# The b21 product of two column pairs, split once more by Strassen's scheme

## The chip, the cores and the metric

The kernel runs on one core of a Trainium2 chip. Its time is the device time of that core in microseconds (us). Three runs of the kernel before took 1364.69 to 1365.26 us, median 1365.02 us.

## What is computed

One layer of a decoder trunk on a sequence of 1024 rows and 1024 features. The input is normalized and modulated (`h`), and one large projection gives all branches; everything is float32.

```python
h = rms_norm(x, norm_w) * (1 + scale) + shift
proj = h @ w_in            # (1024 x 1024) @ (1024 x 11296)
gm_u, gm_v, gm_z, ssm_z, xbc, dt_raw, g_a, g_b = split(proj)
y_a = spatial_gating(gelu(gm_u), gelu(gm_v), ...) * silu(gm_z)
xbc = silu(causal_depthwise_conv(xbc, conv_w, conv_b))
y_b = rms_norm((ssd_scan(...) + xs * d_skip) * silu(ssm_z))
merged = sigmoid(g_a) * (y_a @ w_proj_a) + sigmoid(g_b) * (y_b @ w_proj_b)
out = rms_norm(x + gate * (merged @ w_out), final_norm_w)
```

The change concerns `h @ w_in` alone, and of it the columns other than gm_v, dt_raw and the first two blocks of g_a.

## The kernel before

**Column pairs.** The columns of `w_in` are taken in blocks of 128, two blocks (c1, c2) at a time: 39 pairs. A pair is a matrix product with 2 x 2 blocks: the 1024 contracted rows are halved, the 1024 sequence positions are halved, and the two column blocks are the other side. `pair` (from L590) takes it by seven products in place of eight, with sums of blocks on both sides. The sums of the sequence side (b11, t1, t2, b22, t3, b21, t4; tiles `bop`) are the same for all pairs and stay in SBUF. The sums of the weight side are made for each pair by `pair_weights` (L554) from four loaded quarters: a11, a21, a22, a12 and s1, s2, s4 in eight "ws" buffers.

**Float32 by parts.** Every operand is split into a rounded part and the rest ("h" and "l": a copy on ACT, L571, and a subtraction on DVE, L572), and a product is h x h, h x l and l x h. So `product` (L580) issues 3 x 4 = 12 matmuls of 128 x 128 weights and 512 columns into one PSUM bank. The parts of the weights lie in two rings of eight tiles.

**Order of a pair.** p1, p5, then the p4 of the pair before, p6, p3, p2, p7. p1, p6, p7 and p4 add up in one bank (px), p5 and p3 in another (py), p2 has its own (pz) and uses a12 and b21. ACT copies or DVE adds what stands in a bank into c1 and c2, the results of both column blocks (L601, L637), and then `done1` and `done2` work on them: the convolution (`conv_done`), gates (`z_done`, `gate_done`), or for gm_z and gm_u the "uz" pairs (`zg_done`, `u_done`, L1039 to L1050). The sixteen first pairs are a convolution pair and a uz pair in turn.

**Queues.** Every matmul and every load is kept in the order of the program on its queue (`pin`): PE for matmuls, SP's queue for all loads. Stores go out on ACT's queue. The order on ACT, DVE and POOL is set by a planner with a model of costs; evacuations of PSUM are put ahead (`tc.high_priority`). Side work is hung into a count of products (`later`, `run_tasks`): the mixing weights of the gate, the loads vm (mixing input of a uz pair, `mix_load`), ag and wog (output gates), wbr (weights of the second projection).

**Room.** c1, c2, the convolution's ac, vm, ag and others share six tiles of 128 x 1024, "w4" (`wide`). PSUM in this stage has a px tag of two banks and a "bk" tag of six. After the 37 pairs of `jobs` come two more (`tail`), then the state-space part, the projections and the output. The sequence side's tiles are used again there as room for other tiles.

## Time and profile before

| what | value |
|---|---|
| median of 3 runs | 1365.02 us |
| profiled execution | 1362.27 us |
| its span, first to last instruction | 1360.4 us |
| PE busy | 1347.0 us (99%), 6907 matmuls and transposes |
| weight loads (PEld) | 1114.4 us (82%) |
| DVE busy | 1056.1 us (78%) |
| ACT busy | 800.4 us (59%) |
| POOL busy | 196.1 us (14%) |
| bytes moved by DMA | 288.64 MB, mean 212 GB/s |

PE is TensorE's matmuls, PEld its weight loads (they overlap matmuls), DVE VectorE, ACT ScalarE, POOL GpSimd, SP the queue of loads. The column pairs lie between 143 us and about 905 us of the span. Matmuls are pipelined: the record of one of 512 columns is 389 ns long, and the next one starts 227 ns after it, so the pace is read from the starts. In a row of instructions the columns are start, length, engine, line, operation, output and inputs, shapes and count; behind "[" is the idle time of the engine before it and what ended it. In a row of a group the busy time is followed by the mean length in ns.

### The profile page before, as it was taken

What the parts mean: (1) busy time and instruction counts of PE and PEld (TensorE: products, weight loads), DVE (VectorE), ACT (ScalarE), POOL (GpSimd) and SP (SyncE); (2) the same over time, 40 slices, a digit from 0 to 9 for tenths busy, and PEclk for the clock granted to TensorE, in tenths of its full rate; (3) what the DMA queues carried; (4) which work ended last, traced back from release to release, by engine and by line L of the source; (5) the groups of instructions that cost most, each with busy time, mean ns of one, the idle gap of its engine ahead of it and who ended that gap; (6) DMA issues with size and microseconds to landing.
All of it is one profiled execution on the core that took longest, in us unless ns stands there. A gap on an engine that the chain in (4) does not pass through costs nothing.

```text
span 1360.4 us, 20108 instructions
## 1 busy us (share of the span) xinstructions
PE 1347.0 (99%) x6907; PEld 1114.4 (82%) x6907; DVE 1056.1 (78%) x1731; ACT 800.4 (59%) x1446; POOL 196.1 (14%) x193
## 2 busy tenths in 40 slices
PE   8999999999999999999999999999999999999997
PEld 6688888888888888888888888888888888888886
DVE  4776786787777898688887788358888877959976
ACT  5754666666657665466576655486877834233453
POOL 1000000000000000000000000007798981000002
PEclk9999999999999999999999999999999999999999
DMA  9675444333345667777656866489889878888913
GB/s 292 177 248 142 134 124 124 117 119 122 101 132 155 193 184 231 248 216 246 202 192 193 244 204 186 154 289 318 302 297 311 306 256 291 313 261 317 381 45 124
DMA packets 249577, 288.64 MB, mean 212 GB/s; under 512 B 16860, under 2 KB 196484, under 8 KB 249476
## 3 DMA queue, kind: packets, MB, share of 16 engines
q1 hardware_dynamic: 174868, 203.80, 47.0%
q10 hardware_dynamic: 74544, 83.57, 18.0%
q8 instruction: 54, 0.88, 0.3%
q14 instruction: 47, 0.39, 0.1%
q0 software_dynamic: 64, 0.00, 0.0%
HBM read 199.82 MB, written 87.49 MB: 211 GB/s over the span
## 4 chain that ended last, share of the span: by engine, by line
PE 93%; POOL 3%; DMA 1%; issue 1%; ACT 1%; DVE 1%; SPq 0%; POOLq 0%; DVEq 0%; ACTq 0%
PE xcb L585 6%; PE xz L585 6%; PE xuz L585 6%; PE xx L585 6%; PE xg L585 6%; PE pma L82 5%; PE ox L1914 3%; PE yuz L585 3%; PE yx L585 3%; PE ycb L585 3%; PE yp L1722 3%; PE yz L585 3%; PE vx L990 3%; PE yg L585 3%; PE oy L1914 2%; PE x0p L1722 2%
## 5 line engine op out<-in xcount | busy, mean ns | idle before, releaser
L1159 POOL TENSOR_SCALAR_AFFINE_SELECT dcy<-dcy 128x1024 f32<-128x1024 f32 x32 | 35.3, 1103 | 788.7 <-ACT ea L1155 788.7
L1167 ACT ACTIVATE dcy<-dcy,nacs 128x128 f32<-128x128 f32 x256 | 78.3, 389 | 2.9 <-POOL dcy L1159 2.4
L1183 DVE TENSOR_TENSOR dcy<-dcy,pc 128x1024 f32<-128x1024 f32 x32 | 39.0, 1218 | 8.0 <-PE pc L85 5.8
L1265 POOL TENSOR_TENSOR yz<-y,sl 128x512 f32<-128x512 f32 x32 | 44.7, 1396 | 2.5
L82 PE MATMUL pma<-yh,wah 128*128 128x512 f32 x128 | 43.2, 418 | 0.0
L82 PE MATMUL pma<-yh,wal 128*128 128x512 f32 x128 | 42.6, 413 | 0.0
L82 PE MATMUL pma<-yl,wah 128*128 128x512 f32 x128 | 40.2, 395 | 0.0
L1155 ACT ACTIVATE ea<-dcy 64x512 f32<-64x512 f32 x64 | 39.8, 622 | 0.4
L1190 ACT COPY bn<-pc 128x256 f32<-128x256 f32 x32 | 11.9, 371 | 46.4 <-DVE dcy L1183 44.9
L1060 ACT ACTIVATE ac<-ac 128x1024 f32<-128x1024 f32 x32 | 33.9, 1060 | 8.1 <-DVE ac L1058 7.9
L1264 POOL TENSOR_TENSOR y<-y,ym 128x512 f32<-128x512 f32 (+1 forms) x32 | 37.4, 1170 | 1.8 <-DVE ym L1262 1.8
L1058 DVE SCALAR_TENSOR_TENSOR ac<-c2x,cwt,ac 128x1023 f32<-128x1023 f32 (+2 forms) x24 | 30.7, 1278 | 8.8 <-ACT ac L1056 8.7
L1058 DVE SCALAR_TENSOR_TENSOR ac<-c2cb,cwt,ac 128x1023 f32<-128x1023 f32 (+2 forms) x24 | 30.7, 1278 | 8.2 <-ACT ac L1056 8.0
L1929 POOL TENSOR_TENSOR r<-r,fnw 128x512 f32<-128x512 f32 x4 | 6.1, 1534 | 207.3 <-ACT junk L1927 207.3
L82 PE MATMUL yi<-dcy,xd 128*64 128x128 f32 x512 | 35.0, 279 | 0.0
L1262 DVE TENSOR_TENSOR ym<-yn,ea 128x512 f32<-128x512 f32 (+1 forms) x32 | 19.9, 621 | 18.2 <-PE yn L82 18.0
L1653 DVE SCALAR_TENSOR_TENSOR yn<-yn,par,rb 128x512 f32<-128x512 f32 x32 | 26.1, 822 | 9.1 <-DMA yn<-yb_d 9.1
L82 PE MATMUL sp<-xe,bn 128*128 128x256 f32 x112 | 32.7, 409 | 0.0
L82 PEld LDWEIGHTS yn<-sl,st 128*128 128x128 f32 x224 | 29.8, 191 | 2.8 <-POOL st L1228 0.4
L82 PEld LDWEIGHTS yi<-dcy,xd 128*64 128x64 f32 x512 | 27.3, 136 | 5.7 <-issue 3.2
L1058 DVE SCALAR_TENSOR_TENSOR ac<-c1cb,cwt,ac 128x1023 f32<-128x1023 f32 (+2 forms) x24 | 30.6, 1276 | 1.3 <-ACT ac L1056 1.3
L1022 ACT ACTIVATE vm<-vm,vr 128x128 f32<-128x128 f32 x64 | 25.5, 483 | 10.1 <-DMA vm<-v_d 9.6
(2983 smaller groups left out, 4368.4 us busy)
## 6 DMA issues: line engine op xcount, KB each, us to landing
sl<-s_d SPq DMA_DIRECT2D x32, 768.0 KB
s_d<-ac ACTq DMA_DIRECT2D x32, 512.0 KB
wb_d<-wbb ACTq DMA_DIRECT2D x32, 512.0 KB
dcy<-acs_d SPq DMA_DIRECT2D x32, 512.0 KB
av<-in_w_in_dram SPq DMA_DIRECT2D x36, 256.0 KB
aw<-in_ada_w_dram SPq DMA_DIRECT2D x16, 512.0 KB
wbr<-in_w_proj_b_dram SPq DMA_DIRECT2D x32, 256.0 KB
yb_d<-yz ACTq DMA_DIRECT2D x32, 256.0 KB
```

Of the source, the lines that this page charges most:

```text
L82: pin(PE.matmul(acc, l, r, start=first, stop=last))
L585: pin(PE.matmul(ps, lw[:, k * P : (k + 1) * P], r[k], start=first and n + k == 0, stop=n == 2 and k == 3, skip_group_check=not first))
L990: pin(PE.matmul(ps[pn][j], l[:, j * P : (j + 1) * P], r, start=nm in ("p1", "p5", "p2") and n + units[i][1] == 0, stop=n == 2 and k == 3, ...
L1058: V.scalar_tensor_tensor(ac[:, s:], cc[:, : S - s], conv_wt[:, 3 - s, i : i + 1], ac[:, s:], op0=ALU.mult, op1=ALU.add)
L1155: link("A", lambda: A.activation(ea[hh * HD : (hh + 1) * HD], dcy.rearrange("p (j e) i l -> p e j (i l)", e=2)[hh * HD : (hh + 1) * HD, hh ...
L1159: link("G", lambda: G.affine_select(out=d8, in_=d8, compare_op=ALU.is_ge, fill=-1e30, base=0, pattern=[[0, 2 * HPG], [1, P]], channel_mult ...
L1167: link("A", lambda: A.activation(dcy[:, h, i, :], dcy[:, h, i, :], AF.Exp, bias=sub[:, i, h : h + 1]))
L1183: link("V", lambda: V.tensor_tensor(d3, d3, pc[:, 0:256].unsqueeze(1).to_broadcast([P, HPG, 256]), op=ALU.mult))
L1264: link("G", lambda: G.tensor_add(y1[:, :, t0:], y1[:, :, t0:], m[:, :, t0:]))
L1265: link("G", lambda: G.tensor_mul(yz, y1, sl[:, 4:6]))
L1722: pin(PE.matmul(ps[j], a[:, v, js], r, start=first and n + k == 0, stop=n == 2 and k == KT - 1, skip_group_check=not first))
L1914: pin(PE.matmul(ps, a[:, tsl], b[:, cs], start=first and n + j == 0, stop=n == 2 and j == 3, skip_group_check=not first))
```

## The change

For 34 of the 39 pairs, from the fourth to the 37th, two pairs in a row ("a" and "b", 17 times) share their p2. The a12 of a and the a12 of b stand side by side as a 512 x 256 matrix against b21 (512 x 512). Their product is taken by the same scheme one level down: seven sub-products q1 to q7, each 3 x 2 = 6 matmuls of 256 columns, into three banks (qx, qy and a bank qz) that are added to the halves of a's c1 and b's c1. q1 and q2 come in a after p3; in b q6 and q5 come after p1, q3 and q7 after the p4 of a, and q4 after p3.

- The weight side: p2 of a serves q1 and q2; the sums qa and qb (one tile each) and qc (half a tile) are made in b, four POOL operations of 256 columns and their splits. b's list of parts grows to nine.
- The sequence side: `sub_operands` makes the sub-sums of b21 once, during the first two pairs, on POOL, and stores them (`bq_d`). `sub_load` brings the operand of one sub-product, 128 x 1024 (512 KB), into one of three of b21's four tiles; after each sub-product the load for the one three later is issued on SP's queue.
- b21 itself is stored (`keep_b21`), and loaded again for the last two pairs. Its fourth tile holds the c1 of each a.
- PSUM is divided anew for the pairs: px 2, bk 3, y 1, qx 1, qy 1; and again as before at the tail.
- gm_z and gm_u results may now finish in either order (`uz_done`). In the last two whole pairs p2 comes before p7.
- Where the tiles of b21 served as room later on, they do so now as four tiles of 128 x 1024.

```diff
@@ -65,6 +65,8 @@
+    bq_d = dt_([P, 7, 2, 2, 256], "bq_d")
+    b21_d = dt_([P, 4, S], "b21_d")
@@ -138,7 +140,18 @@
     for nm in BN:
-        bop[nm] = [[hp.tile([P, 512], F32R, name=f"{nm}{v}{k}", tag=f"{nm}{v}{k}") for k in range(4)] for v in "hl"]
+        if nm != "b21":
+            bop[nm] = [[hp.tile([P, 512], F32R, name=f"{nm}{v}{k}", tag=f"{nm}{v}{k}") for k in range(4)] for v in "hl"]
+    def hp_big(name, i, dt=F32R):
+        return hp.tile([P, S], dt, name=name, tag=f"b21_{i}")
+    def b21_tiles(name):
+        tiles = [hp_big(f"{name}{i}", i) for i in range(4)]
+        bop["b21"] = [[t[:, v * 512 : (v + 1) * 512] for t in tiles] for v in range(2)]
+        return tiles
+    b21_first = b21_tiles("b21_")
@@ -533,9 +546,10 @@
                 return psum.tile([P, 512], F32, name=name, tag="px", bufs=2)
-        return psum.tile([P, 512], F32, name=name, tag="bk", bufs=6)
+        return psum.tile([P, 512], F32, name=name, tag="bk", bufs=bank_bufs[0])
     tasks = []
+    bank_bufs = [6]
     slot = [0]
@@ -551,23 +565,41 @@
-    def pair_weights(name, c1, c2):
+    quad = {}
+    def pair_weights(name, c1, c2, role=None):
         a = {}
-        for nm, col, k0 in (("11", c1, 0), ("21", c2, 0), ("22", c2, 4), ("12", c1, 4)):
+        def raw(nm):
+            col, k0 = {"11": (c1, 0), "21": (c2, 0), "22": (c2, 4), "12": (c1, 4)}[nm]
             a[nm] = t = wt(f"a{nm}{name}", "ws", 8, F32)
...
                  w_in[k0 * P : (k0 + 4) * P, col : col + P].rearrange("(k p) c -> p k c", p=P))
-        s1, s2, s4 = (wt(f"s{i}{name}", "ws", 8, F32) for i in (1, 2, 4))
+        def sums():
+            return [wt(f"s{i}{name}", "ws", 8, F32) for i in (1, 2, 4)]
+        for nm in ("11", "21", "22"):
+            raw(nm)
+        if role == "a":
+            s1, s2, s4 = sums()
+            raw("12")
+            quad["a12"] = a["12"]
+        else:
+            raw("12")
+            if role == "b":
+                u = wt(f"u{name}", "ws", 8, F32)
+            s1, s2, s4 = sums()
         s3 = a["21"]
...
             for nm in nms:
-                if nm not in ops:
-                    ops[nm] = wt(f"{nm}{name}h", "wh", 8), wt(f"{nm}{name}l", "wl", 8)
-                (hi, lo), t = ops[nm], parts[nm]
+                t = parts[nm]
+                w = t.shape[-1]
+                ops[nm] = hi, lo = wt(f"{nm}{name}h", "wh", 8)[:, 0:w], wt(f"{nm}{name}l", "wl", 8)[:, 0:w]
                 A.copy(hi, t)
@@ -575,7 +607,16 @@
         V.tensor_sub(s3, a["11"], s3)
-        parts_of("p1", "p5", "p6", "p3", "p2", "p7", "p4")
+        if role == "b":
+            first, lo, hi = quad.pop("a12"), slice(0, 256), slice(256, 512)
+            G.tensor_add(u[:, lo], a["12"][:, lo], a["12"][:, hi])
+            G.tensor_sub(u[:, hi], u[:, lo], first[:, lo])
+            G.tensor_sub(first[:, lo], first[:, lo], a["12"][:, lo])
+            G.tensor_sub(first[:, hi], first[:, hi], u[:, hi])
+            parts.update(qa=u, qb=first, qc=a["12"][:, hi])
+            parts_of("p1", "qa", "p5", "qb", "p6", "p3", "qc", "p7", "p4")
+        else:
+            parts_of("p1", "p5", "p6", "p3", "p2", "p7", "p4")
         return ops
@@ -586,15 +627,68 @@
+    SUBS = (("q1", 0, "p2", 0), ("q2", 1, "p2", 256), ("q6", 4, "qa", 256), ("q5", 3, "qa", 0), ("q3", 2, "qb", 256),
+            ("q7", 5, "qb", 0), ("q4", 6, "qc", 0))
+    SUB = {nm: (w, at) for nm, _, w, at in SUBS}
+    coming_sub, sub_at = [], [0, 0]
+    def sub_load():
+        nm, i, _, _ = SUBS[sub_at[0] % 7]
+        t = hp_big(f"{nm}b{sub_at[0]}", sub_at[0] % 3)
+        sub_at[0] += 1
+        load(f32(t).rearrange("p (v c) -> p v c", v=2), bq_d[:, i].rearrange("p v i c -> p v (i c)"))
+        coming_sub.append((nm, t))
+    def sub_product(nm, ps, ops, first=True, more=True):
+        got, t = coming_sub.pop(0)
+        assert got == nm
+        wnm, at = SUB[nm]
+        wh, wl = ops[wnm]
+        for n, (lw, v) in enumerate(((wh, 0), (wh, 1), (wl, 0))):
+            for k in range(2):
+                pin(PE.matmul(ps, lw[:, at + k * P : at + (k + 1) * P], t[:, v * 512 + k * 256 : v * 512 + (k + 1) * 256],
+                              start=first and n + k == 0, stop=n == 2 and k == 1, skip_group_check=not first))
+        if sub_at[0] < sub_at[1]:
+            sub_load()
+    def sub_operands(i):
+        (h, l), x = bop["b21"], wide(f"bx{i}", F32R)
+        for j in range(2):
+            G.tensor_add(f32(x)[:, j * 512 : (j + 1) * 512], f32(h[i + 2 * j]), f32(l[i + 2 * j]))
+        t = wide(f"bt{i}", F32R)
+        x4, t4 = (f32(w).rearrange("p (a c) -> p a c", a=4) for w in (x, t))
+        G.tensor_sub(t4[:, 0], x4[:, 1], x4[:, 0])
+        G.tensor_sub(t4[:, 1], x4[:, 3], t4[:, 0])
+        G.tensor_sub(t4[:, 2], x4[:, 3], x4[:, 1])
+        G.tensor_sub(t4[:, 3], x4[:, 2], t4[:, 1])
+        for w, nm in ((x, "x"), (t, "t")):
+            hi = wide(f"b{nm}h{i}", F32R)
+            A.copy(hi, f32(w))
+            G.tensor_sub(w, f32(w), f32(hi))
+            for v, part in enumerate((hi, w)):
+                p4 = f32(part).rearrange("p (a c) -> p a c", a=4)
+                if nm == "x":
+                    store(bq_d[:, 0, v, i], p4[:, 0])
+                    store(bq_d[:, 1:3, v, i], p4[:, 2:4])
+                else:
+                    store(bq_d[:, 3:7, v, i], p4)
+    def keep_b21():
+        for k, t in enumerate(b21_first):
+            store(b21_d[:, k], f32(t))
     pending, pairs_done = [], []
-    def pair(name, ops, done1, done2, after=None, whole=False):
+    def pair(name, ops, done1, done2, after=None, whole=False, role=None):
...
         after = after or (lambda n: None)
+        lo, hi = slice(0, 256), slice(256, 512)
@@ -605,12 +699,25 @@
+        def add(c, part, ps):
+            out(V.tensor_add, c[:, part], c[:, part], ps)
+        def own(nm):
+            return psum.tile([P, 512], F32, name=f"{nm}{name}", tag=nm)[:, lo]
         px = psum.tile([P, 512], F32, name=f"x{name}", tag="px", bufs=2)
         product(px, ops["p1"], "b11")
-        c1 = first_c1.pop(name) if name in first_c1 else wide(f"c1{name}")
+        c1 = first_c1.pop(name) if name in first_c1 else hp_big(f"c1{name}", 3, F32) if role == "a" else wide(f"c1{name}")
         out(A.copy, c1[:, 0:512], px)
         after(0)
-        py = bank(f"y{name}")
+        if role == "b":
+            qx, qy = quad["x"], own("qy")
+            sub_product("q6", qx, ops, False)
+            add(quad["c"], hi, qx)
+            sub_product("q5", qy, ops)
+            add(c1, hi, qy)
+            run_tasks()
+        py = bank(f"y{name}") if bank_bufs[0] == 6 else psum.tile([P, 512], F32, name=f"y{name}", tag="y")
         product(py, ops["p5"], "t1")
@@ -618,13 +725,31 @@
             pending.pop()()
+        if role == "b":
+            sub_product("q3", qy, ops, False)
+            add(quad["c"], hi, qy)
+            quad["done"](quad["c"])
+            sub_product("q7", qx, ops, False)
+            add(c1, hi, qx)
         product(px, ops["p6"], "t2", False)
...
         after(3)
-        if not whole:
+        if role == "a":
+            quad.update(x=own("qx"), c=c1, done=done1)
+            sub_product("q1", quad["x"], ops)
+            add(c1, lo, quad["x"])
+            qz = bank(f"z{name}")[:, lo]
+            sub_product("q2", qz, ops)
+            add(c1, lo, qz)
+            run_tasks()
+        elif role == "b":
+            sub_product("q4", qx, ops, False)
+            add(c1, lo, qx)
+            done1(c1)
+        else:
             p2()
@@ -635,10 +760,7 @@
             V.tensor_add(c2[:, 512:1024], c2[:, 512:1024], p5)
-        after(4 if whole else 5)
-        if whole:
-            p2()
-            done1(c1)
+        after(5)
@@ -937,7 +1059,7 @@
-        open_banks()
+        open_banks(ps0, "ps1", 6)
@@ -1036,18 +1158,24 @@
+    half_done = set()
+    def uz_done(g, func):
+        def done(c):
+            A.activation(c, c, func)
+            if g in half_done:
+                V.tensor_mul(c, c, vns[g])
+                store(ya_d[g], c)
+            else:
+                half_done.add(g)
+                V.tensor_mul(vns[g], c, vns[g])
+        return done
     def zg_done(g):
-        def done(cz):
-            A.activation(cz, cz, AF.Silu)
-            V.tensor_mul(vns[g], cz, vns[g])
-        return done
+        return uz_done(g, AF.Silu)
     def u_done(g):
-        def done(cu):
-            A.activation(cu, cu, AF.Gelu_apprx_tanh)
-            V.tensor_mul(cu, cu, vns[g])
-            store(ya_d[g], cu)
-        return done
+        return uz_done(g, AF.Gelu_apprx_tanh)
@@ -1385,8 +1513,12 @@
-        ya_tags[k] = tags = [room.pop(0) for _ in range(4)]
-        yh, yl = ([take(f"y{v}{k}{i}", tags[2 * n + i]) for i in range(2)] for n, v in enumerate("hl"))
+        if k < KT - 2:
+            ya_tags[k] = tags = [room.pop(0) for _ in range(4)]
+            yh, yl = ([take(f"y{v}{k}{i}", tags[2 * n + i]) for i in range(2)] for n, v in enumerate("hl"))
+        else:
+            bigs = [hp_big(f"y{v}{k}", 2 * (k - KT + 2) + n) for n, v in enumerate("hl")]
+            yh, yl = ([t[:, i * 512 : (i + 1) * 512] for i in range(2)] for t in bigs)
@@ -1448,17 +1580,33 @@
-    def open_banks():
+    def open_banks(before, name, n):
         nonlocal ps1, psum
-        ps0.__exit__(None, None, None)
-        ps1 = tc.tile_pool(name="ps1", bufs=1, space=PSUM, reuse_waits="tile")
+        before.__exit__(None, None, None)
+        ps1 = tc.tile_pool(name=name, bufs=1, space=PSUM, reuse_waits="tile")
         psum = ps1.__enter__()
+        bank_bufs[0] = n
+    Q0, NQ = 3, 17
+    roles = {Q0 + 2 * i + j: "ab"[j] for i in range(NQ) for j in range(2)}
+    sub_at[1] = 7 * NQ
     v_block()
+    open_banks(ps1, "ps2", 3)
     ops = pair_weights(*todo[0][:3])
...
             later(5, stats)
+            later(2, keep_b21)
+            for i in range(2):
+                later(3 + 8 * i, sub_operands, i)
+        if n == Q0:
+            for _ in range(3):
+                sub_load()
+        if n == Q0 + 2 * NQ:
+            for k, t in enumerate(b21_tiles("b21again")):
+                load(f32(t), b21_d[:, k])
+        if n == len(jobs):
+            open_banks(ps1, "ps4", 6)
         if n == NPRE:
@@ -1479,7 +1627,7 @@
-            nxt = pair_weights(*todo[n + 1][:3])
+            nxt = pair_weights(*todo[n + 1][:3], roles.get(n + 1))
@@ -1492,7 +1640,7 @@
-            pair(name, ops, d1, d2, None, n == len(jobs) - 1)
+            pair(name, ops, d1, d2, None, n == len(jobs) - 1, roles.get(n))
```

15 lines of the change are left out of this document (9 added, 6 removed).

## The prediction

> **What bounds the kernel now.** I read the page's head first, then the table of stretches (columns: stretch, its length, busy time of PE, weight loads, DVE, ACT and POOL with their counts, granted clock, DMA share, GB/s), then the chain of work in order of time.
>
> ```profile
> span 1360.4 us, 20108 instructions
> PE 1347.0 (99%) x6907; PEld 1114.4 (82%) x6907; DVE 1056.1 (78%) x1731; ACT 800.4 (59%) x1446; POOL 196.1 (14%) x193
> PE 93%; POOL 3%; DMA 1%; issue 1%; ACT 1%; DVE 1%; SPq 0%; POOLq 0%; DVEq 0%; ACTq 0%
> 143.10:183.00 39.90, 39.90 (x191) 33.39 (x190) 31.34 (x63) 25.58 (x44) 1.10 (x1) 1.00 0.40 117
> 183.00:382.00 199.00, 199.00 (x920) 166.28 (x919) 150.73 (x197) 128.98 (x199) 0.00 (x0) 1.00 0.39 118
> 382.00:577.00 195.00, 195.00 (x878) 162.09 (x877) 156.68 (x242) 119.92 (x185) 0.00 (x0) 1.00 0.62 190
> 577.00:857.00 280.00, 280.00 (x1244) 231.92 (x1244) 226.45 (x377) 170.62 (x261) 0.00 (x0) 1.00 0.67 208
> 908.00:1117.00 209.00, 208.85 (x1620) 176.67 (x1619) 173.90 (x300) 146.30 (x382) 171.21 (x163) 1.00 0.88 303
> 154.38 2.72 PE zcb L585 x12
> 157.10 2.72 PE xcb L585 x12
> ```
>
> From 143 to 857 us, where nearly all of the 39 column pairs lie, PE is busy all the time at full clock, and the chain goes from product to product: 12 matmuls, 2.72 us, 226.7 ns each. Only PE time taken out there shortens the kernel, and any wait that PE doesn't have today lengthens it. DVE has 24% idle in the second stretch and 19% in the fourth, POOL nearly everything; DMA is far from full early and at 0.67 in the fourth.
>
> **What it removes and adds on PE.** Two pairs ("a", then "b") lose their product with b21: 24 matmuls of 512 columns. They get seven sub-products of 6 matmuls, 42 matmuls of 256 columns. The kernel has such matmuls already, at its end (weight loads are the PEld rows):
>
> ```profile
> 1350.34 0.39 PE L1914 MATMUL oy<-mwhb,ma11h 128*128 128x512 f32 x1
> 1350.57 0.28 PE L1914 MATMUL ox<-mwhb,ma11h 128*128 128x256 f32 x1
> 1350.68 0.28 PE L1914 MATMUL ox<-wlb,ma11h 128*128 128x256 f32 x1
> ...
> 1353.32 0.28 PE L1914 MATMUL oy<-mwhb,ma11h 128*128 128x256 f32 x1
> 1350.57 0.19 PEld L1914 LDWEIGHTS ox<-wlb,ma11h 128*128 128x128 f32 x1
> 1350.68 0.19 PEld L1914 LDWEIGHTS ox<-mwhb,ma11h 128*128 128x128 f32 x1
> 403.23 1.98 PEld L82 LDWEIGHTS mix<-wst,vm 128*128 128x128 f32 x16
> 405.13 0.77 PEld L585 LDWEIGHTS yuz<-t1h,p5uz6h 128*128 128x128 f32 x4
> ```
>
> The 24 of them start from 1350.57 to 1353.32: 2.75/23 = 119.6 ns each, not the 113.3 that half of 226.7 would be. The loads start as often as the matmuls, and the 16 loads of 128-column matmuls at 403.23 also come at (405.13 - 403.23)/16 = 119 ns: a new weight tile about every 119 ns is the floor. A sub-product is 6 x 119.6 = 0.718 us, seven are 5.02 us; the two old products are 5.44. **Saved: 0.42 us for two pairs, 7.1 us for 17.** Bounds: 113.3 ns gives 4.76 us and 11.6 us saved; the slower look of the other row, 1.98/16 = 124 ns, gives 5.21 and 3.9 us. I take 119.6, which is the same shape.
>
> The Trainium skill, "TensorE: Matmul & The Clock Gate", section "Back-to-back issue gap", has a warm gap of N/2.4 + 2.5 ns: 215.8 and 109.2 ns here, an estimate of 10.1 us saved and a kernel at 1357.1. The rows have 11 ns more at both widths, and the measurement decides.
>
> **DVE, ACT and POOL of two pairs.** The rows by shape (mean ns behind the busy time):
>
> ```profile
> L601 DVE TENSOR_TENSOR c1cb<-c1cb,zcb 128x512 f32<-128x512 f32 x8 | 5.5, 684 | 2.7 <-PE zcb L585 2.7
> L1236 DVE TENSOR_TENSOR st<-st,sp 128x256 f32<-128x256 f32 x48 | 19.9, 414 | 7.3 <-POOL st L1228 5.9 <-PE sp L82 1.0 <-issue 0.2
> L865 DVE TENSOR_TENSOR wbb<-wbr,wbb 128x512 fp32r<-128x512 f32 x32 | 21.9, 683 | 3.2 <-ACT wbb L860 3.0
> L865 DVE TENSOR_TENSOR wba<-wbr,wba 128x256 fp32r<-128x256 f32 x16 | 6.7, 420 | 4.4 <-ACT wba L860 4.4
> L860 ACT CAST wba<-wbr 128x256 fp32r<-128x256 f32 x16 | 6.5, 405 | 19.1 <-DMA wbr<-in_w_proj_b_dram 15.0 <-DVE p2g4l L572 4.1
> L860 ACT CAST wbb<-wbr 128x512 fp32r<-128x512 f32 x32 | 19.8, 618 | 17.0 <-DMA wb_d<-wbb 14.8 <-DVE wbr L876 1.8
> L1228 POOL TENSOR_TENSOR st<-st,cd 128x256 f32<-128x256 f32 x48 | 29.0, 622 | 5.0 <-DVE st L1236 2.8 <-DVE st L1234 2.0
> L1265 POOL TENSOR_TENSOR yz<-y,sl 128x512 f32<-128x512 f32 x32 | 44.7, 1396 | 2.5
> ```
>
> DVE: seven adds of 256 columns for two of 512 (2.90 - 1.37 = +1.53 us), splits qa, qb, qc beside p2's for two p2's (+0.68 + 0.42): +2.6 us in some 38. In the fourth stretch 81% become 88%. ACT +1.0 us, POOL four operations, 2.5 us, where it is idle. Nothing of this lies on PE's path while results leave PSUM in time: the single y bank must be empty before the next p5, with p7, p1 and a sub-product between (at least 6.2 us), and qx and qy have 5.4 us; the add itself takes 0.41 to 0.68. I cost it at nothing. Without that cover each evacuation would cost PE 0.4 to 0.7 us.
>
> **The new loads** are the real price. Each sub-product's b side is a load of 512 KB on SP's queue into one of three buffers, issued when the sub-product three before is done: 119 loads, 62 MB beside 289. That ties SP, which so far ran ahead of PE by about a pair, to PE; weights, vm and ag loads behind them go no earlier. What such loads take:
>
> ```profile
> 343.99 0.34 SPq L91 DMA_DIRECT2D ag<-in_ada_w_dram  x1
> 347.60 1.28 DVE L791 SCALAR_TENSOR_TENSOR gacc<-ag,sc,gacc 128x1024 f32<-128x1024 f32 x1 [1.15 <-DMA ag<-in_ada_w_dram]
> 255.85 0.34 SPq L91 DMA_DIRECT2D vm<-v_d  x1
> 259.69 0.49 ACT L1022 ACTIVATE vm<-vm,vr 128x128 f32<-128x128 f32 x1 [0.44 <-DMA vm<-v_d]
> 262.90 0.69 DVE L574 TENSOR_TENSOR s1uz<-a21uz,a22uz 128x512 f32<-128x512 f32 x1 [2.08 <-DMA a22uz<-in_w_in_dram]
> ```
>
> ag (512 KB) is in use 3.61 us after its issue; behind vm, three weight quarters (0.75 MB) land 3.21 us later, 4.28 us per MB. The order on PE is, in a: p1, p5, old p4, p6, p3, q1, q2, p7; in b: p1, q6, q5, p5, a's p4, q3, q7, p6, p3, q4, p7. Shortest windows: q5's load from q1's end to q5 (q2, p7, p1, q6), 6.9 us against 3.6; q7's from q6's end (q5, p5, p4, q3), also 6.9 us. But q7's load stands behind q3's load, in the first seven quads vm, and the next pair's four weights. Counted from q2's end it needs 3.61 + 2.14 (vm) + 4.28 (weights) + 2.14 (its own 512 KB) = 12.2 us, and PE is there after p7, p1, q6 and those 6.9: 13.0 us. It is hidden by 0.9 us with vm, by 3.0 without, when no stores are in the way. Weights for the next pair have 20 us and more from issue to use, against some 8: hidden.
>
> Bounds of the loss: below, nothing. Above: in the fourth stretch the traffic beside the weights (1.05 MB per 19 us, 55 GB/s) is 153 GB/s, 2.0 MB in those 13 us; all of it ahead of the load would be 8.5 us, 5.5 late, in 7 quads 39 us. The nearest row is the fifth stretch: 303 GB/s, and PE idle 0.15 us of 209. The changed fourth stretch would be at 208 + 3.67 MB/38 us = 305 GB/s. By that row the loss over some 650 us is **0.5 us**, which I take; that stretch looks further ahead than three buffers, so the upper end stays in the range.
>
> **Once only.** At the start POOL builds the sub-operands in two chains, each in four of the six wide tiles: 2 adds (1.40), 4 of 256 columns (0.62), 2 of 1024 (twice 1.40), 10.9 us, and a store, about 3.6 more; with both casts some 16 us. 5.7 MB of stores go with them. The wide tiles are scarce there:
>
> ```profile
> SPq L91 <- DVE wsl L763: 21.9, 1, 21.9
> 171.24 1.22 DVE L763 TENSOR_TENSOR wsl<-wst,wsh 128x1024 fp32r<-128x1024 f32 x1
> 175.95 0.39 PE L82 MATMUL prs<-wsh,ws 128*128 128x512 f32 x1
> 143.24 2.72 PE xcb L585 x12
> 144.49 0.59 ACT L969 COPY vc<-vx 128x512 f32<-128x512 f32 x1
> ```
>
> SP already waits 21.9 us for one of them, and wsl is ready at 172.46, only 3.5 us before PE uses it. Bounds: 0 to 12.5 us (16 - 3.5); I take **1.0**, near the low end, since the chain needs 16 us and its first part starts 20 us ahead of that use. Twice PSUM is divided anew: the first p1 at 143.24 may get a bank that is emptied only at 145.08, so 0 to 1.8 us, and again at the tail; I take **0.7** for both. b21 comes back for the last two pairs: 2 MB, 9 us by the rate above, against p7, p4, p1, p5, p6, p3, 16.3 us: hidden. The p2 that moves forward in the last two pairs costs nothing, being PE work in another order.
>
> **The sum:** 7.1 - 0.5 - 1.0 - 0.7 = 4.9 us less. The profiled execution took 1362.27 us (span 1360.4 and 1.9 around it), so 1357.4; the median of the runs is 2.75 above that execution: **1360.1**.
>
> **The rivals.** A. *q7's load comes late* in the dense stretch. For it: 0.67 share today, 305 GB/s then, a hidden margin of 1 to 3 us. Against: the fifth stretch. Two transfers of 512 KB (4.3 us) between would use up 3.0 and leave 1.3; with other loads beside, 2 us in each of 7 quads is 14 us: 1374. It decides early: 0.13 us per quad more takes the result to no change, 0.45 makes it slower.
> B. *The wide tiles run out at the start* and PE stops in the first three pairs for 6 of the 12.5 us: 1365. At 12.5 it is 1371.6. For it: the 3.5 us; against: a one-time cost, and c1 of each a leaves the wide tiles from the fourth pair on.
> C. *The change doesn't gain what its count says*: a weight load is recorded at 0.19 us, and 42 at 188 ns are 7.9 us, 2.46 more than before; with 17 quads 1409. The loads every 119 ns speak against it. Only the Trainium skill's "Perfetto Trace Analysis", section "Identifying the Most-Contended Engine", which judges TensorE's headroom by weight-load busy time, makes one think of it; the rows show those records overlapping.
> D. *The weight floor doesn't hold*: 113.3 ns, 4.5 us better: 1355.6.
>
> **How the numbers follow.** A measurement of this kernel can tell about 0.2%, 2.7 us, from no change. Forecast 0.50, D 0.04: faster 0.54. B at 6 us 0.19: same 0.19. A 0.22, B at 12.5 0.03, C 0.02: slower 0.27. The forecast's own range is 1355.6 to 1362.3; to hold 8 in 10 it takes in D and B and reaches past A's price: 1354 to 1377.
>
> **What would show it.** Right: six sub-product matmuls in 0.72 us; PE 100% busy in the middle stretches with some 306 matmuls more; DMA share near 0.95 in the fourth; products still at 2.72. Wrong: PE idle before q5 or q7 with a load of the sub-operands as releaser (A); PE idle before 200 us behind wide tiles (B); sub-product matmuls spaced by more than 125 ns (C); PE waiting for DVE at a y, qx or qy bank, which I costed at nothing.

## The result, and the profile after

The changed kernel took **1418.07 us** (median of 4 runs, 1416.63 to 1419.37) where the kernel before took 1365.14 (1364.69 to 1365.26): ratio **1.0388**, 95% interval 1.037 to 1.0406. It is 52.9 us slower; forecast were 4.9 us less. The profiled execution took 1416.83 us, with a span of 1415.1.

The page's head and the table of stretches of the changed kernel (columns as in the prediction's table):

```profile
span 1415.1 us, 21370 instructions
PE 1356.9 (96%) x7213; PEld 1128.4 (80%) x7213; DVE 1114.2 (79%) x1850; ACT 812.5 (57%) x1484; POOL 296.6 (21%) x277
PE 62%; DMA 8%; DVE 7%; issue 3%; ACT 2%; POOL 1%; SPq 1%; ACTq 0%; POOLq 0%; DVEq 0%
```
```profile
143.10:183.00 39.90, 34.68 (x152) 28.12 (x153) 32.82 (x60) 23.90 (x40) 10.21 (x7) 0.91 0.56 165
183.00:382.00 199.00, 187.00 (x907) 156.87 (x906) 151.31 (x215) 125.17 (x200) 28.88 (x24) 0.97 0.61 197
382.00:577.00 195.00, 190.48 (x956) 161.64 (x955) 168.71 (x251) 118.60 (x188) 23.17 (x20) 1.00 0.75 242
577.00:857.00 280.00, 267.90 (x1303) 225.57 (x1303) 234.24 (x411) 162.84 (x259) 31.13 (x28) 0.99 0.89 294
```

PE, which had no idle time between 143 and 857 us, now has 5, 12, 4.5 and 12 us of it in the four stretches, and the granted clock is below 1 in three of them. PE's busy time rose by 10 us although it has less to do. The chain of waits, 93% PE before, is 62% PE. Whom PE waited for between 143 and 908 us, where it had no wait before: the eight costliest rows of the view of waits (total, times, longest):

```profile
PE xuz L626 <- ACT c2uz L695: 6.3, 1, 6.3
PE qyx L650 <- DMA q5b<-bq_d: 5.5, 1, 5.5
PE xcb L626 <- ACT p1cb0h L603: 4.1, 1, 4.1
PE xcb L626 <- ACT c1cb L695: 3.5, 4, 1.7
PE qxuz L650 <- DMA q7b<-bq_d: 3.1, 2, 1.6
PE qyx L650 <- DVE c1x L695: 2.2, 1, 2.2
PE qxz L650 <- DMA q7b<-bq_d: 1.9, 1, 1.9
PE qxg L650 <- DMA q7b<-bq_d: 1.8, 1, 1.8
```

There is no single culprit: sub-operands that land late (the four DMA rows, 12.3 us), copies and adds out of PSUM that are late (ACT and DVE at L695), and two single long waits early (6.3 us before xuz at 205 us, 4.1 us before the first pair). The sub-products themselves run as counted (timeline of the changed kernel):

```profile
251.71 0.64 PE L650 MATMUL qxuz<-q7b,qbcb1h 128*128 128x256 f32 x4
252.19 0.40 PE L650 MATMUL qxuz<-q7b,qbcb1l 128*128 128x256 f32 x2
252.43 1.09 PE L626 MATMUL xcb<-t2h,p6cb1h 128*128 128x512 f32 x4
```

Six matmuls in 252.43 - 251.71 = 0.72 us.

### The profile page after: what moved, and what is told of

The parts are those of the page before. It is cut to its first block, busy times and chain, and to the rows that moved or that the text cites. A ratio compares the mean times of both kernels' runs of the same rounds, so it can differ in the third digit from the quotient of the medians.

```text
span 1415.1 us, 21370 instructions
## 1 busy us (share of the span) xinstructions
PE 1356.9 (96%) x7213; PEld 1128.4 (80%) x7213; DVE 1114.2 (79%) x1850; ACT 812.5 (57%) x1484; POOL 296.6 (21%) x277
## 4 chain that ended last, share of the span: by engine, by line
PE 62%; DMA 8%; DVE 7%; issue 3%; ACT 2%; POOL 1%; SPq 1%; ACTq 0%; POOLq 0%; DVEq 0%
PE pma L84 5%; PE xz L626 4%; PE xx L626 4%; PE xcb L626 3%; PE xuz L626 3%; PE xg L626 3%; PE yp L1872 3%; PE ox L2066 3%; PE yi L84 2%; PE yz L626 2%; PE yx L626 2%; PE sp L84 2%; PE yuz L626 2%; PE yg L626 2%; PE yn L84 2%
## 5 line engine op out<-in xcount | busy, mean ns | idle before, releaser
L612 POOL TENSOR_TENSOR ux<-a12x 128x256 f32<-128x256 f32 x6 | 8.6, 1436 | 217.4 <-DVE a21x L609 143.8
L612 POOL TENSOR_TENSOR ucb<-a12cb 128x256 f32<-128x256 f32 x6 | 8.8, 1474 | 212.6 <-DVE a21cb L609 179.2
L84 PE MATMUL pma<-yh,wah 128*128 128x512 f32 x128 | 43.2, 418 | 0.0
L1390 DVE TENSOR_TENSOR ym<-yn,ea 128x512 f32<-128x512 f32 (+1 forms) x32 | 19.9, 623 | 19.3 <-PE yn L84 19.3
L1186 DVE SCALAR_TENSOR_TENSOR ac<-c1x,cwt,ac 128x1023 f32<-128x1023 f32 (+2 forms) x24 | 30.7, 1281 | 3.8 <-ACT ac L1184 2.9
L982 ACT CAST wbb<-wbr 128x512 fp32r<-128x512 f32 x32 | 19.8, 619 | 22.9 <-DMA wb_d<-wbb 17.2
```

The costliest lines, as they stand in the source:

```text
L84: pin(PE.matmul(acc, l, r, start=first, stop=last))
L1186: V.scalar_tensor_tensor(ac[:, s:], cc[:, : S - s], conv_wt[:, 3 - s, i : i + 1], ac[:, s:], op0=ALU.mult, op1=ALU.add)
```

## The experiments

The kernel before took 1365.1 us beside the changed kernel and 1361.5 to 1362.5 us beside the experiments, so each result stands as its distance to the runs of the kernel before that were taken with it, on one chip. The changed kernel stands at +52.9. The 95% intervals of the ratios reach 0.1 to 0.4% to each side, 1.5 to 6 us, so smaller differences between two kernels rest on their traces. A "quad" is two pairs, a and b, with their seven sub-products; "the chains" are the two rows of POOL work that build the sub-operands at the start, with their stores.

| kernel | us | above before |
|---|---|---|
| e1 once-only parts, no quads | 1392.0 | +30.0 |
| f1 e1 without the chains | 1378.2 | +16.4 |
| f2 f1, PSUM as before | 1376.4 | +14.6 |
| f3 f2, b21 not stored and reloaded | 1373.0 | +11.2 |
| f4 f3, last products as before | 1365.2 | +3.4 |
| e2 all but the loads | 1394.1 | +32.0 |
| e3 loads of 32 KB | 1394.7 | +32.7 |
| g1 loads of 256 KB | 1415.1 | +53.6 |
| e5 no chains, loads from b21 | 1421.3 | +59.2 |
| g3 chains, loads from b21 | 1434.3 | +72.8 |
| g2 no chains, no loads | 1380.6 | +19.1 |
| e4 weight sums on DVE | 1428.6 | +67.1 |
| h1 sub-products spread | 1434.3 | +72.7 |
| h3 e2, spread | 1404.8 | +43.2 |
| h4 chains' stores by POOL | 1422.7 | +61.1 |
| h2 h1, h4 and last products | 1439.5 | +77.9 |
| i1 four buffers | 1432.0 | +69.5 |
| i2 i1 and last products | 1430.4 | +67.9 |

### Once-only parts, or the quads?

e1 makes no quads and loads no sub-operands, but builds and stores them, divides PSUM anew and stores and reloads b21:

```diff
-    Q0, NQ = 3, 17
+    Q0, NQ = 3, 0
...
```

> The changed kernel with no pair in the a or b role: p2 of every pair as before, and of the change only what is done once (the two POOL chains and their stores, b21 stored and loaded again, PSUM divided anew, the tiles of b21 as four large ones). The changed kernel is 20 us behind already when its fourth pair starts. Theory 'early room' (the once-only parts take the wide tiles and tie up ACT and SP): about 1388 us, 20 to 25 above the kernel before, lost before 225 us of the span. Theory 'quads alone' (the once-only parts are harmless, what the first three pairs lose comes from the planner's other order for the quads): 1364 to 1368.

+30.0 us, ratio 1.0218 (1.0188 to 1.0248). I had costed these parts at 1.7 us. In its trace the fourth pair starts 19.8 us later than before, nothing is lost from there to the last pair of the main part, and some 10 us go at the tail. So a loss of more than half of the changed kernel's comes about without any sub-product. Four nested kernels then took the parts away one after the other.

f1, without the chains:

```diff
-            for i in range(2):
-                later(3 + 8 * i, sub_operands, i)
```

> The once-only parts alone (no quads), and of these without the two chains that build the sub-operands and their stores; the rest as in the run of the once-only parts (1392.0 us, 30 us above before). Theory 'the chains': nearly all of the 16 us that the once-only parts lose between the first and the fourth pair is theirs, so about 1378 us, and the fourth pair starts 4 to 6 us later than before instead of 19.8. Rival 'the round trip': the 2 MB of b21 stores and the reload in front of the fourth pair make it wait, then it stays at 1388 to 1392.

f2, also without dividing PSUM anew (both calls of open_banks in the loop's code left out):

> As f1, and PSUM isn't divided anew: six shared banks and two px banks all through. Theory 'the divided banks': the 4.25 us before the first pair's p1 and part of the loss behind the last pair are waits for all the banks of the pool that closes; then 4 to 6 us less than f1, about 1373, and p1 of the first pair starts as before (143.1). Rival 'late weights': the first pair's weights come late for another reason (SP's queue behind something else), the 4.25 us stay, and it is f1 within 1.5 us.

f3, also without keep_b21 and without the reload:

> As f2, and b21 is neither stored nor loaded again. Theory 'the chains': stores and reload were hidden, so within 1.5 us of f2. Rival 'the round trip': 2 us and more below f2, since 4 MB pass at the time when the first pairs' weights are loaded.

f4, also with p2 behind p7 in the last two pairs:

```diff
-        else:
+        elif not whole:
             p2()
...
-        after(5)
+        after(4 if whole else 5)
+        if whole:
+            p2()
+            done1(c1)
```

> As f3, and the last two pairs take p2 behind p7 again, as the kernel before did. Theory 'the last p2': p2 between p7 and p4 covered the copy of px out of its bank, and PE waits 0.84, 0.84 and 1.93 us at the p4s of the last pairs without it: 2.5 to 4 us below f3, and no such waits. Rival 'nothing': p2 is PE work in another order, the same within 1 us. What stays above 1362 after that belongs to the changed room at the tail and to the planner's order.

**By the times of the runs: chains 13.6 us, PSUM 1.8, b21's trip 3.4, last products 7.8, and 3.4 (1.0027; 1.0016 to 1.0038) that stay.** The chains' theory held. Of PSUM's part the place was right: PE's wait of 4.1 us before the first pair's p1 (weights cast late; the row with p1cb0h above) is gone in f2. But f2 and f3, like g1 and e4, have a wait at x3p (a product of a projection, well behind the pairs) that e1, f1, f4 and both kernels don't have, and which I didn't explain. In f2 (first row) and in f3:

```profile
PE x3p L1864 <- DVE tha L1666: 3.1, 1, 3.1
PE x3p L1860 <- DVE tha L1662: 2.0, 1, 2.0
```

The wait in f2 is followed by 6.8 us with a granted clock of 0.50, the one in f3 by none: around x3p f2 loses 6.3 us and f3 2.4. All three steps next to these runs contain that. The starts of the products ahead of it (up to the first x2p) divide the loss in another way: chains 14.4, **PSUM 7.0, b21's trip nothing (f2 is 5.1 us behind the kernel before there, f3 5.3), last products 5.6.** So f2's expectation, 4 to 6 us for the banks, was nearer than its time says. And 'the round trip', which by the times would have won with 3.4 us, isn't shown: the 3.4 us stand at x3p, the fourth pair, ahead of which b21 is loaded again, is as late in f2 as the first (0.9 us behind before), and one of f2's four runs took 1373.2 us, as f3 did. What stays in f4 stands behind the last matmul: that starts 0.9 us earlier than before, and the kernel ends 2.8 us later. f4's expectation puts it down to the changed room at the tail and the planner's order; that wasn't taken apart.

For the last products I had read half as much from the waits; f3's rows between 850 and 935 us, all gone in f4:

```profile
PE xg L626 <- DVE c2g L695: 1.8, 1, 1.8
PE yi L84 <- issue: 1.5, 1, 1.5
PE yn L84 <- POOL st L1356: 0.7, 1, 0.7
PE xz L626 <- ACT c2z L695: 0.7, 1, 0.7
```

The first and the last are p4 behind p7: both work on px, and p4 must wait until px is copied. p2 between them had covered that.

### The quads without their traffic

e2 makes all sub-products, but loads only the first three sub-operands and uses them again (so the products are of other data). e3 adds a load of 32 KB where each load was.

```diff
+        if sub_at[0] < 3:
             t = hp_big(f"{nm}b{sub_at[0]}", sub_at[0] % 3)
             load(f32(t).rearrange(...), bq_d[:, i].rearrange(...))
+            kept_sub.append(t)
+        t = kept_sub[sub_at[0] % 3]
...
```

> The changed kernel, but after the first three sub-operands nothing is loaded: every later sub-product reads one of those three tiles again (the product with b21 is then wrong for 34 pairs), so 116 loads of 512 KB and SP's waits for sub-products are gone. Theory 'loads' (traffic, or SP bound to PE): the 27 us lost from the fourth pair to the last go, and 4 of the 7 us that PE saves show: 1385 to 1392. Theory 'engines' (POOL sums, evacuations and splits in ACT's and DVE's order cost PE the time): 1412 to 1418.

> As the run without the loads, but each later load is issued at its place, with its wait for the sub-product, and brings 64 columns (32 KB) in place of 1024: SP stays bound to PE, the traffic of 59 MB is gone (the same product is wrong). Theory 'traffic': as without loads, 1385 to 1392. Theory 'bound order' (weights and side loads stand behind SP's wait): as the changed kernel, 1412 to 1418.

Both are 2 to 3 us above e1, where 7.1 below was counted. So the quads lose 9 us without any traffic, **the loads 20.9 more** (+52.9 against +32.0; by the traces, 24.1 between the fourth and the 37th pair), and tying SP to PE costs next to nothing by itself: e3, whose loads do that, is 0.7 us above e2, whose don't. Where the 9 us go can be read from starts of successive matmuls in e2's trace: 5.6 us stand at the start of p7, in seven pairs. p7 must wait until ACT has copied p6's result from px. Between them stood p3 and p2, 5.44 us; in b, q4 in p2's place leaves 2.72 + 0.72 = 3.44, in a q1 and q2 leave 4.16. Four of the seven places are in a b (4.1 us), three in an a (1.5). Another 1.2 us stand before one q2, which waits for an add of DVE. The times of e1 and e2 lie within each other's intervals; by the starts, e2 loses 0.9 us between the fourth and the 37th pair, where it should gain 7.2.

### Bytes, place, or order?

e5 leaves the chains out, and loads from the stored b21:

> The changed kernel without the two POOL chains at the start and their 3.7 MB of stores; the sub-products' loads of 512 KB stay, but they read the stored b21 (the product with b21 is then wrong for 34 pairs). Theory 'early room': the 20 us of the first three pairs go, 1396 to 1401. Theory 'the planner's order': no change, 1415 to 1420.

It came out 6 us above the changed kernel, though its fourth pair started 13.7 us earlier: as if the middle gave back whatever the start won. Two runs tested that. g2 leaves out chains and loads; g3 has the chains, and e5's loads:

```diff
-        load(f32(t).rearrange(...), bq_d[:, i].rearrange(...))
+        load(f32(t), b21_d[:, i % 4])
```

> The changed kernel without the two chains and without the loads after the third. Theory 'two separate losses': the chains' 13.8 us (the once-only parts with and without them: 1392.0 and 1378.2) go, from the 1394.1 us without loads: about 1380. Rival 'one bound in the middle': the chains' loss is only an earlier form of what the middle stretch takes anyway, as without the chains but with loads (1421.3); then it stays at 1390 or more.

> The changed kernel, chains and all, but each sub-operand load takes 512 KB from the stored b21 instead of the stored sub-operands (the same bytes, rows of 4 KB with 16 KB between them instead of 28; the products are of other data). That is also what the run without the chains did, which took 1421.3. Theory 'the same bytes': 1416 to 1420, and the run without chains lost in the middle what it had won early for a reason of its own. Rival 'the place of the rows': loads from rows 16 KB apart are slower, 1428 to 1438, and then the 13.8 us of the chains are in truth separate.

The chains cost 32.0 - 19.1 = 12.9 us without loads, 72.8 - 59.2 = 13.6 with e5's loads, 13.6 without quads. They are **a loss of their own that adds up with the rest**; 'one bound in the middle' fell. And loads of the same size, in packets of 4 KB in both, from rows 16 KB apart cost 19.9 us more than from rows 28 KB apart (12.2 of it, by the traces, between the fourth and the 37th pair).

g1 halves each load; the other half of each buffer stays as it was:

> The changed kernel with each sub-operand load after the third cut to its first half, 256 KB instead of 512 KB, into the three buffers that stay (the lower parts of the b side are then stale). With 32 KB it took 1394.7 us, with 512 KB 1418.1. Theory 'the bytes': DMA time that is taken from other transfers, in proportion to the bytes: about 1406 us. Rival 'the knee': the transfers have room until the share nears 1, so half of the bytes cost little: 1396 to 1400. Rival 'late in the queue': a load of any real length comes late behind the weights' loads on SP's queue, 1410 and more.

+53.6: as slow as with all the bytes. By the time of the run 'the bytes' and 'the knee' fell. But in its trace 17.9 us are lost between the fourth pair and the last pair of the main part, against 25.0 in the changed kernel and 1.7 in e3; another 4.8 go around the x3p wait, so the equality is partly chance. Over e3, half of the bytes cost 16.2 us there and all of them 23.3; in proportion to the bytes it would have been some 11. Late sub-operands are nearly gone there, other waits have come. From the view of waits of g1, 205 to 890 us (the chains' 6.3 us before xuz, which come first there, left out):

```profile
PE xz L626 <- ACT c1z L700: 3.2, 3, 2.1
PE xcb L626 <- ACT c1cb L700: 3.1, 2, 2.2
PE qyx L655 <- DVE c1x L700: 2.2, 1, 2.2
PE qxz L655 <- DVE c1z L700: 2.1, 1, 2.1
PE qxg L655 <- DMA q2b<-bq_d: 1.3, 1, 1.3
```

e4 moves the four sums of 256 columns from POOL to DVE (G. to V. in four lines):

> The changed kernel with the four sums of 256 columns, which make the weights of q5, q6, q3, q7 and q4, on DVE instead of POOL. Theory 'the shared port': beside POOL's sums DVE's operations take longer (1.76 us instead of 1.28 in one place, 1.22 instead of 0.68 in another), and POOL's own take 1.2 to 2.3 us instead of 0.62; DVE then has 1.7 us more per two pairs, but no stretched ones: 2 to 6 us below 1418. Rival 'not on the path': the same within 1.5 us. Rival 'DVE full': 2 us and more above.

14 us worse than with POOL (8.3 between the fourth and the 37th pair, 4.3 around the x3p wait): 'DVE full' holds. POOL's sums are indeed long, 1.13 us in the mean of all 68 (0.74 to 2.34) instead of the 0.62 that I took. Two of their groups (changed kernel, groups by shape, 183 to 908 us):

```profile
L612 POOL TENSOR_TENSOR ucb<-a12cb 128x256 f32<-128x256 f32 x6 | 8.8, 1474 | 212.6 <-DVE a21cb L609 179.2 <-ACT wba L982 33.3
L613 POOL TENSOR_TENSOR ux<-ux,a12z 128x256 f32<-128x256 f32 x3 | 3.2, 1068 | 0.2
```

The Trainium skill, "SBUF — State Buffer", section "SBUF: two separate sides", has DVE and GpSimd lock one pair of ports against each other; the longer sums agree. Whether they cost PE anything the run doesn't show; it shows that DVE has no room for them.

### Three ways to mend it, none of which did

h1 sets the sub-products apart in b (p1, q6, p5, q5, a's p4, q3, p6, q7, p3, q4, p7), h3 does the same without loads. h4 issues the chains' stores from POOL (nc.gpsimd.dma_start for store in sub_operands), h2 is h1, h4 and the last products together.

> The changed kernel with the same products, bytes and buffers, but in b the sub-products stand apart: p1, q6, p5, q5, a's p4, q3, p6, q7, p3, q4, p7. The load of q5 and of q7 then has 9.6 us from its buffer's release to its use instead of 6.9 (worked out from 2.72 and 0.72 us products), and p7 comes 4.2 us after p6's end instead of 3.4. Theory 'short windows': q5 and q7 come late for 13.6 us in all and p7 waits 6.1 us for the copy of its bank; most of that goes: 1400 to 1408. Rival 'the bytes': what the loads take from other transfers stays, and the waits come out somewhere else: 1414 and more.

> Without the loads after the third (1394.1 us), and in h1's order. Theory 'the copy's cover': the 5.6 us that PE waits at p7 for ACT's copy of the bank are what the sub-products lose without traffic, and most go: 1388 to 1390. Rival 'elsewhere': 1393 and more.

> The changed kernel with the chains' stores issued by POOL instead of ACT. Theory 'ACT held': ACT's queue stands at stores that wait for POOL's parts (the fourth pair's copy behind them came 6.3 us late, with 3.4 us of halved clock after it), so 6 to 9 us below 1418: 1409 to 1412. Rival 'wide tiles': the chains hold four wide tiles and other work waits for those; then within 2 us of 1418.

> As h1, the chains' stores issued by POOL, which makes their data, instead of ACT, and in the last pair of the main part and the very last one q4 or p2 stands behind p7 again. If the three mechanisms are separate: 13 us for the order, 6 to 9 us for the stores, 4 to 8 us for the last products, together about 1392 (1388 to 1398). If the loss is one bound of the middle, 1405 and more. It is still above before either way.

None was faster: +20, +11, +8 and +25 us against the kernels that they alter (h3 against e2, the others against the changed one), and the favoured theories fell. The rivals of h1, h2 and h3 had no upper end, and so hold without saying much; h4's, within 2 us of 1418, is missed by 2.7 us. In h1 no q7 comes late any more (q5 and q4 do once each, 2.5 and 2.0 us) and hardly a p7 waits, but with one product between two sub-products of one bank PE waits for the add between them, even in h3 without traffic. Why that add is late shows in h1's timeline around one q4 (DVE's rows, and PE's):

```profile
256.27 0.40 PE L650 MATMUL qxuz<-q7b,qbcb1l 128*128 128x256 f32 x2
...
257.91 1.23 DVE L1169 TENSOR_TENSOR c1uz<-c1uz,ya 128x1024 f32<-128x1024 f32 x1 [1.15 <-ACT c1uz L1167]
...
259.05 0.68 DVE L604 TENSOR_TENSOR p6uz2l<-s2uz,p6uz2h 128x512 fp32r<-128x512 f32 x1
...
259.65 0.41 DVE L695 TENSOR_TENSOR c1cb<-c1cb,qxuz 128x256 f32<-128x256 f32 x1
...
260.12 0.74 PE L650 MATMUL qxuz<-q4b,qccb1h 128*128 128x256 f32 x4 [0.70 <-DVE c1cb L695]
```

q7's last matmuls start at 256.27. Its add takes 0.41 us and starts 3.4 us later, because DVE works in order and had two other operations first, one of which waited 1.15 us for ACT. The add's own duration, which I used, is the small part.

What holds the fourth pair is a tile, rather than the place of the chains' stores in ACT's queue. In the changed kernel:

```profile
200.56 0.54 ACTq L96 DMA_DIRECT2D s_d<-ac  x1
204.27 0.59 ACT L695 COPY c2uz<-xuz 128x512 f32<-128x512 f32 x1 [2.81 <-DMA s_d<-ac]
204.91 1.65 PE L626 MATMUL xuz<-t4h,p4uz0h 128*128 128x512 f32 x3 [6.26 <-ACT c2uz L695]
```

The copy out of px writes c2uz, a wide tile, whose last owner (ac) is still being stored. The chains hold four of the six wide tiles, and PE waits until a store has landed. With POOL issuing the chains' stores (h4) that wait was not shorter but 11.8 us, in another form: the copy stood on ACT behind work on vm, ACT waited 6.0 us for vm's load, and SP had waited 15.4 us for a store of an ac before it could issue that load.

i1 gives the sub-operands a fourth buffer, with four loads ahead in place of three, and a's c1 a wide tile instead; i2 also restores the last products:

```diff
-        t = hp_big(f"{nm}b{sub_at[0]}", sub_at[0] % 3)
+        t = hp_big(f"{nm}b{sub_at[0]}", sub_at[0] % 4)
...
-        c1 = ... hp_big(f"c1{name}", 3, F32) if role == "a" else wide(f"c1{name}")
+        c1 = ... wide(f"c1{name}")
```

> The changed kernel in its own order, with the fourth of the b21 buffers used for sub-operands too, and a's c1 in a wide tile instead of there. The shortest time from a buffer's release to its use then is four products and three sub-products, 13.0 us, where q5 and q7 had 6.9 (the load took 5.3 us in the median before q7, 8.0 at most, and up to 7.4 us of waiting in SP's queue). The copies keep the order and the cover that they have. Theory 'short windows': the waits for late sub-operands, 13.6 us, go and nothing takes their place: 1402 to 1407. Rival 'the bytes': these waits go, and as much comes up at other places, since the same 62 MB delay other transfers and ACT and DVE stand behind those: 1413 to 1420. Rival 'the wide tiles': c1 over two pairs takes a wide tile that others wait for: above 1420.

> As i1, and q4 of the last pair of the main part and p2 of the very last pair stand behind p7 again. Theory 'the last products': the once-only parts gained 7.8 us by that, so 6 to 8 us below i1; rival 'the tail is bound otherwise under this order': within 2 us of i1. Above 1362 in either case.

In i1's trace PE waits for no sub-operand at all any more, and the kernel is 17 us slower than the changed one: 'the wide tiles' holds. One place shows the mechanism in both traces. The changed kernel:

```profile
373.07 0.59 ACT L695 COPY c1x<-xx 128x512 f32<-128x512 f32 x1 [1.84 <-DMA s_d<-ac]
373.76 0.42 DVE L695 TENSOR_TENSOR c1x<-c1x,qyx 128x256 f32<-128x256 f32 x1
374.23 1.22 PE L650 MATMUL qyx<-q3b,qbx2h 128*128 128x256 f32 x4 [2.21 <-DVE c1x L695]
```

and i1:

```profile
375.19 0.34 SPq L93 DMA_DIRECT2D ag<-in_ada_w_dram  x1
378.90 1.28 DVE L913 SCALAR_TENSOR_TENSOR gacc<-ag,sc,gacc 128x1024 f32<-128x1024 f32 x1 [0.88 <-DMA ag<-in_ada_w_dram]
380.21 0.58 ACT L695 COPY c1x<-xx 128x512 f32<-128x512 f32 x1
381.31 0.41 DVE L695 TENSOR_TENSOR c1x<-c1x,qyx 128x256 f32<-128x256 f32 x1
381.78 1.01 PE L650 MATMUL qyx<-q3b,qbx2h 128*128 128x256 f32 x3 [4.75 <-DVE c1x L695]
```

In the changed kernel a store of ac that lands late holds a wide tile; the copy of p1's result waits for that tile; the add of q5 waits for the copy; q3 waits for the add. In i1 the tile goes through one more hand: SP waits 6.9 us for a store of ac before it can load ag (375.19), DVE works on ag until 380.18, and only then can the copy have ag's tile. It costs 2.2 us in the one kernel and 4.8 in the other, where c1 lies in wide tiles over two pairs. i2 is within 2 us of i1, and the runs of each differ by more (1426.6 to 1432.3 and 1425.7 to 1432.2): by its trace 2.0 us are won between the main part's last pair and the first pma product, and more was lost ahead of it.

No version beat the kernel before.

## Why the prediction was wrong

| step | forecast, us | measured, us | from |
|---|---|---|---|
| 34 x 12 long matmuls for 119 x 6 short ones | -7.1 | -7.2 | starts in the trace after |
| the quads without traffic; of it 5.6 before p7 | 0 | +9.2 | e2 less e1 (+2.0), less the gain |
| loads of the sub-operands | +0.5 | +20.9 | after less e2 |
| chains at the start | +1.0 | +13.6 | e1 less f1 |
| PSUM divided anew | +0.7 | +1.8 (by starts 7.0) | f1 less f2 |
| b21 stored and loaded again | 0 | +3.4 (by starts 0) | f2 less f3 |
| products of the last two pairs moved | 0 | +7.8 (by starts 5.6) | f3 less f4 |
| the end, behind the last matmul | not named | +3.4 | f4 less before |
| sum | -4.9 | +52.9 | |

The measured column adds up because its steps lead from the kernel before to the changed one. "By starts" is what the traces show ahead of the x3p wait, which the changed kernel doesn't have. That a part costs the same in the changed kernel as where it was measured is shown for the chains (three settings), and nearly for the last products (from the last pair of the main part to the first pma product: 3.0 us from f3 to f4, 2.0 from i1 to i2). PSUM's wait of 4.1 us before the first pair stands in the changed kernel too.

**Right: the pace.** 0.72 us for six matmuls; C (188 ns) and D (113.3) are out. The Trainium skill's formula, "TensorE: Matmul & The Clock Gate", section "Back-to-back issue gap", would have had 109.2 ns, the gap of a single matmul by itself as the page says; these rows have 120, and deciding by the row was right.

**Wrong: "I cost it at nothing".** I compared the time between two uses of a bank with the duration of the add, 0.41 to 0.68 us. What counts is when the add's turn comes: 3.4 us after its matmuls in the row above. And I gave p7 no line of its own. In b its cover went from 5.44 to 3.44 us by q4 taking p2's place; the prediction names covers only for the y, qx and qy banks. The sign to look for, "PE waiting for DVE at a y, qx or qy bank", came true at qy in the changed kernel (2.2 and 0.3 us) and at qx in e2 (0.9 us), and ACT's copies of px came on top.

**Wrong: the loads by "the nearest row", the fifth stretch.** That stretch moves 303 GB/s without loss, but with its data asked for long ahead. I saw that, and took its 0.5 us all the same. Rival A had the right place: q5 and q7 late, 12.3 us in five waits against the 14 in seven that it priced. The longest is not the load's own slowness: SP waited 11.0 us for DVE's work on wbb before it could load wbr, and q5's load stood behind that. Its buffer was free when q1 ended, at 642.4 us; from the changed kernel's timeline:

```profile
642.01 0.40 PE L650 MATMUL qxz<-q1b,p2z2l 128*128 128x256 f32 x2
648.29 1.22 SPq L93 DMA_DIRECT2D wbr<-in_w_proj_b_dram  x2
649.60 0.69 SPq L93 DMA_DIRECT2D q5b<-bq_d  x1
654.83 1.23 PE L650 MATMUL qyx<-q5b,qax5h 128*128 128x256 f32 x4 [5.53 <-DMA q5b<-bq_d]
```

The prediction counted what stands behind a sub-load on SP's queue, not what a sub-load stands behind. But g1 and i1, in which these waits nearly or wholly vanish, are no faster, though g1's middle is 7.1 us shorter. The other way by which the loads reach PE is stores that land later, wide tiles that come free later, and ACT and DVE in order behind them. Traces show this at single places; how the 20.9 us divide between the ways was not measured, and why half of the bytes cost 16.2 of 23.3 us in the middle stays open.

**Wrong: "I take 1.0, near the low end"** for the chains. The bounds, 0 to 12.5, nearly held the 13.6. Rival B even named the wait (PE idle behind wide tiles), and its 12.5 us got a chance of 0.03. Two conditions stood in the profile: SP waiting 21.9 us for such a tile, and 3.5 us of room. Both spoke for the upper end.

**Wrong: "I take 0.7 for both"** (PSUM divided anew). The 1.8 us that bounded it counted the time until a bank is empty. PE's wait there was 4.1 us, for weights that were cast late, and half a clock behind it; by the starts it is 7.0 us with the tail.

**Wrong: "The p2 that moves forward in the last two pairs costs nothing, being PE work in another order."** It was the cover of a copy: 5.6 us by the starts, 7.8 by the times.

**Wrong: the form of the range.** A, B and the PSUM covers stood as alternatives with a price each, and the range reached to the dearest. They have separate places (start, middle, tail), and for the chains the runs show that they add up: 13 to 14 us in three settings. The forecast with A's 14 us and B's other 11.5 would have been 1386, and the covers come on top.

## What to carry to other kernels

Where an engine is 99% busy, every product in its order is also the cover of somebody's copy: before a product is moved, shortened or taken away, list for each bank, tile and queue what the time between release and use was and becomes, and set it against how late the copy's turn comes, not against its duration. Mishaps in separate places are terms of one sum and not rivals. A scarce buffer that something already waits for (here the wide tiles) should be priced at the upper end.

## What the runs showed of the hardware that was not expected

**Waits cost twice.** After several of PE's waits the granted clock is 0.50 for 3.4 us or a multiple. The changed kernel's stretches right after two of them (the last figure but two is the clock):

```profile
146.79:152.07 5.28, 5.28 (x12) 4.01 (x13) 5.18 (x12) 1.24 (x2) 1.85 (x3) 0.50 0.42 115
374.20:377.60 3.40, 3.37 (x14) 3.27 (x15) 1.65 (x3) 3.35 (x5) 0.00 (x0) 0.50 0.23 31
```

The 12 matmuls of the first, 512 columns wide, take 5.28 us instead of 2.72; added up over the matmuls' starts between 143 and 960 us it is 9.1 us. It is a good part of why PE's busy time rose. The Trainium skill, "TensorE: Matmul & The Clock Gate", section "HAM oscillation — how this bites in real kernels", sets the limit at gaps of about 3.4 us; the second stretch follows a wait of 2.2 us, while the waits of 1.8 and 1.9 us in the rows above were followed by no lower clock. How long PE stood does not decide alone: of its idle times in the traces of all twenty kernels (from 140 to 1330 us), 9 of 67 between 1.5 and 2.0 us were followed by a clock of 0.50, 6 of 16 up to 2.5, 8 of 12 up to 3.0, 9 of 11 up to 3.5, and all 41 longer ones.

**Where a load's rows lie counts.** 512 KB from rows of 4 KB that start 16 KB apart, in place of 28 KB, cost 19.9 us more over 119 loads (g3). Their time from issue to landing was up to some 1 us longer: by the trace's DMA packets, taken in the order of their starts, 4.2 us in the median before q5 instead of some 3.2, and 5.3 instead of 4.2 before q3. Whether the distance does it or the place of the two tensors in memory was not tested.
